# A decoder layer on one core: the last expert stage rebuilt, with V rows in fp32 in place of two-part sums at every third step

## The chip, the cores and the metric

The kernel runs on one core of a Trainium2 chip. The metric is the device time of one execution in microseconds (us); the figure of a kernel is the median of its runs. The profile is of one execution and gives times from the start of its span.

## What is computed

One step of a hybrid decoder layer for 1024 prompt tokens and 8 sample tokens: a mixer of two recurrent branches, an attention to 256 memory tokens, and a product-key expert layer (PEER), each added to the residual, then a final norm. The change touches the last part alone. For each token and each of 8 heads the 16 best of 16384 experts are picked, so 128 picks per token:

```python
idx  = ...                                # [token, 8 heads, 16 picks], from the two halves' scores
gate = softmax(top_s)
act  = gelu(einsum('td,thkd->thk', xb, expert_u[idx]))
coef = gate * act
out  = einsum('thk,thkd->td', coef, expert_v[idx])        # then x + out, RMSNorm
```

`expert_u` and `expert_v` are tables of 16384 rows of 1024 fp32 numbers (4 KB a row, 64 MB a table).

## The kernel before, in words

**Order.** The 1024 tokens are 8 blocks of 128, two to a group. `front(gi)` does all of a group up to its picks; `experts` (L1556) does the expert layer of the group before, beside it. The program is written in one order, and a planner at build time gives each engine a fixed list of instructions: where several are ready in its own model of time, the one that is earlier in the program goes first, and one that is ready may pass one that is not. At run time every engine goes through its list in order.

**The U side.** `u_step` (L1521) gathers, for one pick of each of 128 tokens, 128 rows of U into a buffer "U" by an indirect DMA that GpSimd issues (L1498), and multiplies and sums them with the tokens on VectorE (`dot`, L1502). In the fronts four picks of 16 are multiplied on GpSimd instead; in the tail all are dots on VectorE. A batch of 16 picks ends with Gelu and the gate; the factors are `cf`. So a block is 128 gathers.

**The V side, in two ways.** Blocks 0 to 3 go by gathers: `v_step` (L1534) gathers 128 V rows and adds them, times the factor, to `acc` on VectorE (L1550). Blocks 4 to 7 go in pairs by the whole table: `spread` (L1571) makes a matrix `cmat` [expert, token] of the factors, and `dense_sum` (L1612) multiplies it with the table in 128 steps of 128 V rows.

In `spread` there are 64 iterations of four tokens each for a pair. An iteration makes two 0/1 matrices by comparing a row of numbers with the picks' row and column numbers: `ra` on ScalarE (L1593, L1594) or VectorE (L1596) by turns, `rb` on VectorE (L1600), and GpSimd multiplies `rb` with the factors (`gtt`, L125). Four fp32 matmuls of 128x128 follow into a PSUM buffer "pp", and ScalarE copies the result to `cmat`. `cmat` is 128 KB per partition and has one buffer.

In `dense_sum` a step loads 128 V rows (0.5 MB, "Vx", issued by SyncE), splits the step's part of `cmat` and each half of the V rows in two float32r parts (ScalarE copies, L122; VectorE subtracts, L1626 and L1631; for one half of every second step GpSimd subtracts, L125), and adds three products for each of two halves and two blocks: 12 matmuls with 512 columns. The sums stay in four PSUM buffers ("pc", "pp").

**The tail.** The V rows of block 3 are left over for it (`beside`). After the last `front`, its pools are closed (`fronts.close`, L1724) and two pools are opened over their memory: `rows_late` with "U" (4 buffers), "Vx" and "cs", and `wd` with `cmat`, "vs" and "by". A tile of them waits until all of the old pool under it is released. Then the program is

```python
cmat = spread(late[:2])                   # blocks 4, 5
late += experts(prompts(chosen))          # U gathers and dots of blocks 6, 7
dense_sum(late[:2], cmat, ())
for z, k in beside[:VPOS]: v_step(...)    # 16 V steps of block 3
dense_sum(late[2:], spread(late[2:]), beside[VPOS:])     # blocks 6, 7; 112 V steps, one before each step
```

Blocks 6 and 7 get their picks at the end of the last `front` (`Best.pairs`, tile q3b).

Of the kernel before, what the change touches and what calls it, by code (L numbers as in the profile page):

```python
# [16 lines left out]
P = 128  # L17
D = 1024
NS = 8                      # sample tokens
# [6 lines left out]
NQ3, NG4, NXA, NK1, NU, NUT, NVX, NVS, NW, NAC = 26, 6, 2, 5, 5, 4, 4, 6, 3, 1  # L26
# [5 lines left out]
SPLIT = (0,)              # groups that go on by single blocks after their scans  # L32
POOL_DOTS = (2, 6, 10, 14)
NEARLY = 0
VPOS = 16
LATE_SLOTS = ()
ACT_A = range(0, 32, 2)
POOL_B = range(0, 32)
PB = 16                     # picks per batch of the expert phase
# [9 lines left out]
def decode_layer(ctx, tc, I, O):  # L49
    nc = tc.nc  # L50
    kept = ctx.enter_context(tc.tile_pool(name="kept", bufs=1))       # constants of every phase
    we = ctx.enter_context(tc.tile_pool(name="we", bufs=1))           # the experts' buffers
    fronts = ctx.enter_context(ExitStack())                           # what the fronts alone need
    rows_of = fronts.enter_context(tc.tile_pool(name="rows_of", bufs=1))      # gathered rows
# [44 lines left out]
    def pp():  # L99
        return pst("pp", 2)  # L100
# [26 lines left out]
    # ---------------------------------------------------------------- constants  # L127
# [6 lines left out]
    triu = const.tile([P, P], F32, name="triu")          # [k, l] = 1 for k <= l  # L134
    G.affine_select(out=triu, in_=ones, compare_op=OP.is_ge, fill=0.0, base=0,
                    pattern=[[1, P]], channel_multiplier=-1)
    maskg = const.tile([P, 2, 64], F32, name="maskg")    # [i mod 64, {i < t, i <= t}, t]
# [9 lines left out]
    sel4 = const.tile([P, 2, 32], F32, name="sel4")      # head of a channel in a pair of channel tiles  # L147
# [4 lines left out]
    sel4t = const.tile([P, 2, P], F32, name="sel4t")     # the same transposed, for every 32 partitions  # L152
# [5 lines left out]
    blk8 = kept.tile([P, NS], F32, name="blk8")         # [p, t] = 1 for p // 16 == t  # L158
# [15 lines left out]
    # parameters of a channel each, by columns  # L174
# [41 lines left out]
    V.tensor_scalar(alog, alog, -1.0, None, op0=OP.mult)     # a_head  # L216
# [8 lines left out]
    # state kept from group to group  # L225
    st = const.tile([P, D], F32, name="st")              # SSD, [n, (head, p)]
    G.memset(st, 0.0)
    rst = const.tile([P, 8, 64], F32, name="rst")        # RWKV, [(head of a pair, k), pair, v]
    G.memset(rst, 0.0)
    TT = [const.tile([P, 8, 64], F32, name=f"TT_{i}") for i in range(2)]     # inverses, transposed  # L230
# [7 lines left out]
    # kept in memory  # L238
# [7 lines left out]
    # ---------------------------------------------------------------- pieces  # L246
# [13 lines left out]
    class Parts:  # L260
        """1024 rows as the sum of two parts that float32r carries: 8 slices [128, n] of each."""
# [9 lines left out]
    def parts(wt):  # L271
        """Weights as the sum of two parts."""
# [8 lines left out]
    def three(out, a, b, first, last):  # L281
        """a.T @ b of operands in two parts."""
        for i, (x, y) in enumerate(((a[0], b[0]), (a[0], b[1]), (a[1], b[0]))):
            mm(out, x, y, first and i == 0, last and i == 2)

    def to_cols(x, n, dst, t0, wname=None):
        """x [n, 1024] into dst, 4 tiles [128, 2, T], by channels."""
# [38 lines left out]
    # ---------------------------------------------------------------- memory keys and values  # L326
    def memory():
        """By buffers of the experts, which are free until the first of them are chosen."""
        def cols4(dst, x, b):
            """x [128, 1024] into dst, by channels, with the norm's weights."""  # L330
# [54 lines left out]
    # ---------------------------------------------------------------- front of a group  # L385
# [6 lines left out]
    class Best:  # L392
        """The 16 best pairs of keys and their gates, for n rows and nh heads of each."""

        def __init__(self, n, nh):
# [9 lines left out]
                                   for i in range(2))                       # over i  # L405
# [8 lines left out]
        def add(self, sc, h):  # L414
            """Scores [n, 2 x 128] of head h."""
            for j in range(2):
                self.top16(sc[:self.n, j * P:(j + 1) * P], self.s[:self.n, h, j, :], self.i[:self.n, h, j, :])
# [32 lines left out]
    def front(gi):  # L450
        b0, nb = GROUPS[gi]
        sa, sm, sc_ = gi == 0, gi == 1, gi == 2     # the sample's input projection; up to its queries; the rest of it
# [7 lines left out]
        # normalized input, by channels  # L460
# [19 lines left out]
        # z, as 2 silu(z)  # L480
# [21 lines left out]
        # step widths  # L502
# [9 lines left out]
        def softplus(n, s):  # L512
            """dt of columns s (blocks) and n rows."""
# [23 lines left out]
        # causal convolution, by channels  # L537
        hc = t("hc", [P, 12, 3], 1)                      # what the rows before the group add to its first three
# [46 lines left out]
        # SSD scan  # L585
# [99 lines left out]
        # RWKV: projections, decayed operands by pairs of heads  # L685
# [24 lines left out]
        wc = t("wc", [P, 8, TMAX // 64], 2)              # decay of a whole chunk  # L710
# [21 lines left out]
        for q in range(4):  # L732
# [18 lines left out]
            for j in range(2):  # L751
# [4 lines left out]
                                       op0=OP.mult, op1=OP.mult)            # -kk  # L756
# [3 lines left out]
            V.scalar_tensor_tensor(ta[:, :, :TP], ta[:, :, :TP], 1.0, kk[:, :, :TP], op0=OP.add, op1=OP.mult)   # -2 b  # L760
# [22 lines left out]
            for j in range(2):  # L783
# [5 lines left out]
                for s in range(2):               # even heads (k, b), odd heads (b, k)  # L789
# [8 lines left out]
            # the triangles to invert  # L798
# [19 lines left out]
        # inverses of the triangles' diagonal blocks, a block to a partition  # L818
# [951 lines left out]
```

## Time and profile before

| | us |
|---|---|
| median of 3 runs (5183.37 to 5193.70) | 5188.58 |
| span of the profiled execution | 5188.6 |
| VectorE busy | 3990.9 (77%) |
| TensorE busy (matmuls) | 3838.1 (74%) |
| GpSimd busy | 3073.8 (59%) |
| ScalarE busy | 1864.4 (36%) |
| DMA, mean of the span | 251 GB/s |

The profiled execution's own time is its span. Engines: PE is TensorE (PEld its weight loads), DVE VectorE, ACT ScalarE, POOL GpSimd. A group names line, engine, operation and the tiles written and read; its columns are the count, the busy time, the mean of one in ns, and the idle time of the engine just before it with what ended most of that. The clock is TensorE's granted clock, 1.00 for 2.4 GHz and 0.50 for 1.2 GHz, as a mean of the stretch. An fp32 matmul stands in the trace as two instructions.

### The profile page before, as it was taken

What the parts mean: (1) busy time and instruction counts of PE and PEld (TensorE: products, weight loads), DVE (VectorE), ACT (ScalarE), POOL (GpSimd) and SP (SyncE); (2) the same over time, 40 slices, a digit from 0 to 9 for tenths busy, and PEclk for the clock granted to TensorE, in tenths of its full rate; (3) what the DMA queues carried; (4) which work ended last, traced back from release to release, by engine and by line L of the source; (5) the groups of instructions that cost most, each with busy time, mean ns of one, the idle gap of its engine ahead of it and who ended that gap; (6) DMA issues with size and microseconds to landing.
All of it is one profiled execution on the core that took longest, in us unless ns stands there. A gap on an engine that the chain in (4) does not pass through costs nothing.

```text
span 5188.6 us, 62002 instructions
## 1 busy us (share of the span) xinstructions
PE 3838.1 (74%) x20264; PEld 3063.8 (59%) x20264; DVE 3990.9 (77%) x7461; ACT 1864.4 (36%) x4475; POOL 3073.8 (59%) x2282
## 2 busy tenths in 40 slices
PE   7889867687977856978687467866756998047889
PEld 6677756565755734766566345655645776046667
DVE  4662397988766799887669987775799999689885
ACT  4544312232332212424332234243244554035445
POOL 2120045766767566567666776777667666678662
PEclk8988878888768868985788678758876999556999
DMA  3242778888878988997888678868825999865985
GB/s 96 91 129 85 230 250 305 271 288 288 275 241 313 320 278 296 306 311 229 314 326 265 227 256 273 271 221 301 283 71 177 350 348 329 275 202 190 308 285 166
DMA packets 586859, 1302.42 MB, mean 251 GB/s; under 512 B 80236, under 2 KB 326408, under 8 KB 586528
## 3 DMA queue, kind: packets, MB, share of 16 engines
q0 software_dynamic: 223488, 813.79, 45.3%
q1 hardware_dynamic: 363048, 484.67, 28.2%
q8 instruction: 160, 2.62, 0.2%
q14 instruction: 163, 1.34, 0.1%
HBM read 1268.49 MB, written 29.90 MB: 250 GB/s over the span
## 4 chain that ended last, share of the span: by engine, by line
PE 31%; DVE 30%; DMA 13%; issue 11%; POOL 9%; ACT 5%; SPq 1%; POOLq 0%; DVEq 0%; another core or an unknown queue 0%; ACTq 0%
PE pp L116 17%; PE pc L116 10%; DVE U L1502 6%; DMA U<-in_expert_u_dram,idx 5%; POOL U L1498 5%; DVE acc L1550 4%; DMA U<-in_expert_v_dram,idx 4%; POOL vs L125 2%; DVE q3b L438 2%; POOL U L125 1%; PE pv L116 1%; DVE vs L1600 1%; DMA w<-in_w_in_dram 1%; PE pg L116 1%; DVE q3b L441 1%
## 5 line engine op out<-in xcount | busy, mean ns | idle before, releaser
L1498 POOL DMA_INDIRECT U<-in_expert_u_dram,idx x1024 | 1215.9, 1187 | 745.3 <-DVE act L1502 245.7
L1502 DVE CUSTOM_DVE_ANT_0 U<-U,xa 128x1024 f32<-128x1024 f32 x840 | 1149.8, 1375 | 281.0 <-DMA U<-in_expert_u_dram,idx 264.6
L1498 POOL DMA_INDIRECT U<-in_expert_v_dram,idx x512 | 644.6, 1259 | 416.1 <-DVE acc L1550 117.9
L1550 DVE SCALAR_TENSOR_TENSOR acc<-U,cf,acc 128x1024 f32<-128x1024 f32 x512 | 748.2, 1461 | 167.3 <-DMA U<-in_expert_v_dram,idx 155.3
L116 PE MATMUL pp<-qw,w 128*128 128x256 f32 (+2 forms) x3024 | 764.8, 397 | 121.2 <-issue 43.4
L116 PE MATMUL pp<-w,qw 128*128 128x256 f32 (+1 forms) x2624 | 661.8, 401 | 151.0 <-DVE g L1040 40.6
L116 PEld LDWEIGHTS pp<-qw,w 128*128 128x128 f32 x3024 | 602.8, 210 | 242.2 <-issue 97.2
L116 PEld LDWEIGHTS pp<-w,qw 128*128 128x128 f32 (+1 forms) x2624 | 504.0, 195 | 279.5 <-DVE g L1040 47.7
L116 PE MATMUL pc<-vs,cs 128*128 128x512 f32 x1536 | 529.2, 398 | 78.1 <-POOL vs L125 46.6
L116 PE MATMUL pp<-vs,cs 128*128 128x512 f32 x1536 | 517.2, 391 | 0.0
L125 POOL TENSOR_TENSOR U<-U,xa 128x1024 f32<-128x1024 f32 x192 | 463.8, 2416 | 39.8 <-DMA U<-in_expert_u_dram,idx 36.8
L1526 ACT ACTIVATE U<-U 128x1024 f32<-128x1024 f32 x192 | 202.4, 1054 | 595.8 <-POOL U L125 588.5
L116 PEld LDWEIGHTS pc<-vs,cs 128*128 128x128 f32 x1536 | 282.7, 188 | 176.5 <-POOL vs L125 70.5
L125 POOL TENSOR_TENSOR vs<-Vx,vs 128x512 fp32r<-128x512 f32 x128 | 221.4, 1729 | 198.1 <-ACT vs L122 193.8
L122 ACT ACTIVATE vs<-Vx 128x512 fp32r<-128x512 f32 x512 | 304.4, 622 | 95.0 <-PE pp L116 93.9
L116 PEld LDWEIGHTS pp<-vs,cs 128*128 128x128 f32 x1536 | 289.1, 188 | 59.7
L116 PE MATMUL pp<-vs,vs 128*128 128x128 f32 x1024 | 231.0, 404 | 120.0 <-POOL vs L125 107.6
L1631 DVE TENSOR_TENSOR vs<-Vx,vs 128x512 fp32r<-128x512 f32 x384 | 296.0, 795 | 13.2 <-ACT vs L122 7.5
L116 PEld LDWEIGHTS pp<-vs,vs 128*128 128x128 f32 x1024 | 204.5, 299 | 146.5 <-POOL vs L125 141.6
L1626 DVE TENSOR_TENSOR cs<-cmat,cs 128x256 fp32r<-128x256 f32 x256 | 147.7, 577 | 106.6 <-ACT cs L122 102.1
L278 POOL TENSOR_TENSOR w<-w,U 128x1024 fp32r<-128x1024 f32 x31 | 74.5, 2403 | 258.2 <-ACT U L122 218.2
L122 ACT ACTIVATE cs<-cmat 128x256 fp32r<-128x256 f32 x256 | 106.9, 418 | 311.1 <-PE pp L116 293.7
(489 smaller groups left out, 7138.9 us busy)
## 6 DMA issues: line engine op xcount, KB each, us to landing
Vx<-in_expert_v_dram SPq DMA_DIRECT2D x256, 512.0 KB
w<-in_w_in_dram SPq DMA_DIRECT2D x124, 1024.0 KB
w<-in_w_pq_dram SPq DMA_DIRECT2D x40, 1024.0 KB
w<-in_w_out_dram SPq DMA_DIRECT2D x20, 1024.0 KB
w<-in_w_mq_dram SPq DMA_DIRECT2D x20, 1024.0 KB
w<-in_w_mo_dram SPq DMA_DIRECT2D x20, 1024.0 KB
U<-in_expert_u_dram,idx POOLq DMA_INDIRECT x1024
q<-kt_d SPq DMA_DIRECT2D x40, 256.0 KB
```

What stands on the lines that cost most here:

```text
L116: T.matmul(out, a, b, start=first, stop=last)
L122: S.activation(out, in_, AF.Copy, scale=scale if scale is not None else 1.0)
L125: G.tensor_tensor(out, a, b, op=op)
L278: (V if i else G).tensor_tensor(lo[:, k4, :], wt[:, k4, :], hi[i].bitcast(F32), op=OP.subtract)
L438: V.tensor_tensor(oh[:n], iota50[:n, None, :].to_broadcast([n, 8, NCAND]), posf[:n, h, k8].unsqueeze(2).to_broadcast([n, 8, NCAND]), op=OP ...
L441: V.tensor_reduce(idf[:n, h, k8], oh[:n], axis=AX.X, op=OP.add)
L1498: G.indirect_dma_start(out=dst, out_offset=None, in_=table, in_offset=bass.IndirectOffsetOnAxis(ap=idx, axis=0))
L1502: V.tensor_tensor_reduce(out=u, in0=u, in1=x, scale=1.0, scalar=0.0, op0=OP.mult, op1=OP.add, accum_out=out)
L1526: S.activation(u, u, AF.Copy, accum_out=z["act"][:, k:k + 1])
L1550: V.scalar_tensor_tensor(z["acc"], v, cf, z["acc"], op0=OP.mult, op1=OP.add)
L1626: V.tensor_tensor(cl[:, :nt], cmat[:, c, :nt], ch[:, :nt].bitcast(F32), op=OP.subtract)
L1631: (gtt if hf and c % 2 else lambda *a: V.tensor_tensor(*a[:3], op=a[3]))(vl, v[:, s], vh.bitcast(F32), OP.subtract)
```

## The change

- `NEARLY` 0 to 40: 40 V steps of block 3 stand before `fronts.close`, and use the fronts' five "U" buffers. `VPOS` 16 to 24: 24 more stand between the dense sums, and 64 beside the second.
- `experts` of blocks 6 and 7 stands before the first `spread`.
- `NUT` 4 to 5 buffers "U" in the tail; "by" moves to `rows_late`; both pools get `reuse_waits="tile"`: a tile waits for the old tiles that lie under it alone.
- `spread`: `rb` is made by four tensor_scalar of 128x128 on VectorE (compare and multiply in one), without GpSimd; the matmuls go to the PSUM buffers "tp" and "pg" by turns.
- `dense_sum`: in every third step (43 of 128) `cmat` and the V rows go into four plain fp32 matmuls, with no split; in the others VectorE does all subtractions.
- Comments are removed, with no effect on the program.

```diff
-NQ3, NG4, NXA, NK1, NU, NUT, NVX, NVS, NW, NAC = 26, 6, 2, 5, 5, 4, 4, 6, 3, 1
+NQ3, NG4, NXA, NK1, NU, NUT, NVX, NVS, NW, NAC = 26, 6, 2, 5, 5, 5, 4, 6, 3, 1
-NEARLY = 0
-VPOS = 16
+NEARLY = 40
+VPOS = 24
-POOL_B = range(0, 32)
+SPLIT_V = 3
@@ spread
-                p = pp()
-                if t0 // 4 in POOL_B:
-                    V.tensor_tensor(rb, iota[:, None, :].to_broadcast([P, 4, P]),
-                                    by[:, 1, t0:t0 + 4].unsqueeze(2).to_broadcast([P, 4, P]), op=OP.is_equal)
-                    gtt(rb, rb, by[:, 2, t0:t0 + 4].unsqueeze(2).to_broadcast([P, 4, P]), OP.mult)
-                else:
-                    for a in range(4):
-                        V.tensor_scalar(rb[:, a, :], iota, by[:, 1, t0 + a:t0 + a + 1], by[:, 2, t0 + a:t0 + a + 1],
-                                        op0=OP.is_equal, op1=OP.mult)
+                for a in range(4):
+                    V.tensor_scalar(rb[:, a, :], iota, by[:, 1, t0 + a:t0 + a + 1], by[:, 2, t0 + a:t0 + a + 1],
+                                    op0=OP.is_equal, op1=OP.mult)
+                p = tp() if t0 // 4 % 2 else pg()
@@ dense_sum
+            if c % SPLIT_V == 0:
+                for hf in range(2):
+                    for b in range(len(blocks)):
+                        mm(acc[b][hf], cmat[:, c, b * P:(b + 1) * P], v[:, hf * 512:(hf + 1) * 512], c == 0, c == P - 1)
+                continue
-                (gtt if hf and c % 2 else lambda *a: V.tensor_tensor(*a[:3], op=a[3]))(vl, v[:, s], vh.bitcast(F32),
-                                                                                       OP.subtract)
+                V.tensor_tensor(vl, v[:, s], vh.bitcast(F32), op=OP.subtract)
@@ program
-    rows_late = ctx.enter_context(tc.tile_pool(name="rows_late", bufs=1))     # not less than rows_of
-    for tag in ("U", "Vx", "cs"):
+    rows_late = ctx.enter_context(tc.tile_pool(name="rows_late", bufs=1, reuse_waits="tile"))
+    for tag in ("U", "Vx", "cs", "by"):
         pools[tag] = rows_late
-    pools["wd"] = ctx.enter_context(tc.tile_pool(name="wd", bufs=1))
-    cmat = spread(late[:2])
+    pools["wd"] = ctx.enter_context(tc.tile_pool(name="wd", bufs=1, reuse_waits="tile"))
     late += experts(prompts(chosen))
-    dense_sum(late[:2], cmat, ())
+    dense_sum(late[:2], spread(late[:2]), ())
```

## Rows read from the trace of the kernel before

**Rows 1.** Windows: PE, PEld, DVE, ACT, POOL busy (count), clock, DMA, GB/s
```profile
3780.00:3924.00 144.00, 89.54 (x402) 68.95 (x402) 143.47 (x420) 68.49 (x163) 87.68 (x71) 0.73 0.11 36
3924.00:4000.00 76.00, 45.87 (x192) 40.88 (x192) 70.34 (x88) 36.55 (x84) 65.64 (x52) 0.55 0.65 214
4000.00:4398.00 398.00, 364.00 (x1539) 281.39 (x1539) 366.10 (x600) 199.96 (x403) 243.94 (x199) 1.00 0.96 347
4398.00:4578.00 180.00, 0.00 (x0) 0.00 (x0) 119.42 (x197) 1.81 (x7) 114.34 (x97) 0.50 0.80 270
4578.00:4765.00 187.00, 128.94 (x549) 112.73 (x550) 175.73 (x161) 101.89 (x231) 154.20 (x111) 0.58 0.49 154
4765.00:5045.00 280.00, 234.17 (x976) 181.02 (x976) 243.83 (x285) 120.27 (x243) 188.96 (x121) 0.99 0.89 304
5045.00:5173.00 128.00, 126.75 (x564) 104.22 (x563) 71.20 (x117) 73.09 (x140) 31.02 (x24) 1.00 0.57 181
```

**Rows 2.** Timeline (start us, us, engine): last picks, first gather
```profile
3922.30 0.18 DVE L442 CAST idx<-q3b 128x64 int32<-128x64 f32 x1
3924.13 1.25 POOL L1498 DMA_INDIRECT U<-in_expert_u_dram,idx  x1
```

**Rows 3.** Groups of stage B: count, busy us, mean ns, idle before
```profile
L1502 DVE CUSTOM_DVE_ANT_0 U<-U,xa 128x1024 f32<-128x1024 f32 x131 | 160.0, 1222 | 2.7 <-DMA U<-in_expert_u_dram,idx 2.6
L1631 DVE TENSOR_TENSOR vs<-Vx,vs 128x512 fp32r<-128x512 f32 x192 | 128.3, 703 | 2.5
L1626 DVE TENSOR_TENSOR cs<-cmat,cs 128x256 fp32r<-128x256 f32 x128 | 92.1, 720 | 26.2 <-ACT cs L122 24.3
```

**Rows 4.** Waits of stage C: us in total, times, longest us
```profile
DVE U L1502 <- DMA U<-in_expert_u_dram,idx: 59.5, 75, 2.6
POOL U L1498 <- DVE act L1502: 49.4, 52, 2.1
```

**Rows 5.** Waits of stage E, while V rows are gathered
```profile
PEld pc L116 <- POOL vs L125: 59.8, 37, 2.1
```

**Rows 6.** Timeline of TensorE: the last matmuls of the second dense sum
```profile
5175.44 0.61 PE L116 MATMUL pp<-vs,cs 128*128 128x512 f32 x2
```

**Rows 7.** Groups of stage D, the second factor matrix
```profile
L125 POOL TENSOR_TENSOR vs<-vs,by 128x512 f32<-128x512 f32 x61 | 93.1, 1532 | 10.3 <-DVE vs L1600 9.6
L1600 DVE TENSOR_TENSOR vs<-iota,by 128x512 f32<-128x512 f32 x61 | 67.8, 1123 | 0.6 <-issue 0.6
L1596 DVE TENSOR_TENSOR vs<-niota,by 128x512 f32<-128x512 f32 x31 | 36.1, 1164 | 0.5 <-PE pp L116 0.5
L1550 DVE SCALAR_TENSOR_TENSOR acc<-U,cf,acc 128x1024 f32<-128x1024 f32 x45 | 68.0, 1511 | 0.0
L116 PE MATMUL pp<-vs,vs 128*128 128x128 f32 x512 | 121.7, 416 | 49.0 <-POOL vs L125 41.5 <-DVE xa L1643 3.7 <-ACT vs L1594 3.7
```

**Rows 8.** Groups of stage E, while V rows are gathered
```profile
L1631 DVE TENSOR_TENSOR vs<-Vx,vs 128x512 fp32r<-128x512 f32 x120 | 115.9, 988 | 0.1
L1550 DVE SCALAR_TENSOR_TENSOR acc<-U,cf,acc 128x1024 f32<-128x1024 f32 x83 | 110.4, 1330 | 0.9 <-DMA U<-in_expert_v_dram,idx 0.9
```

**Rows 9.** Groups of VectorE in the whole span: tensor_scalar from SBUF, alone
```profile
L704 DVE TENSOR_SCALAR q<-q 128x256 f32<-128x256 f32 x4 | 1.2, 288 | 0.5 <-ACT q L703 0.5
L1580 DVE TENSOR_SCALAR vs<-idx 128x128 int32<-128x128 int32 x4 | 0.8, 212 | 0.0
```

**Rows 10.** Tiles cmat and vs: minimum, median, maximum ns
```profile
L1626 DVE TENSOR_TENSOR cs<-cmat,cs x256: 408/425/1504, 4003.0 to 5170.9; 128x256 fp32r<-128x256 f32 x128
L1631 DVE TENSOR_TENSOR vs<-Vx,vs x384: 675/685/2423, 3999.9 to 5171.5; 128x512 fp32r<-128x512 f32 x192
```

**Rows 11.** Timeline of weight loads of fp32 matmuls with 512 columns
```profile
3794.03 0.09 PEld L116 LDWEIGHTS pv<-U,dgs 128*8 128x8 f32 x1 [0.34 <-issue]
3794.46 0.09 PEld L116 LDWEIGHTS pv<-U,dgs 128*8 128x8 f32 x1 [0.34 <-issue]
```

**Rows 12.** Windows of tile q3b, the picks: DVE, ACT, POOL busy
```profile
3780.00:3924.00 144.00, 72.69 (x324) 0.00 (x0) 30.02 (x24) 0.73 0.11 36
```

## The prediction

> **What bounds the kernel now.** I read the page first, for its span and its slices, then the windows of the tail, then in each window the groups and the waits. The profiled execution took 5188.6 us, and the median of the three runs is 5188.58 us, so the sum below is made against the one number. The edits begin where the picks of the last two blocks are being made, about 3780 us, so only 1409 us are in play [rows 1]. I call the stages A to E:
>
> A, 3780 to 4000: the first factor matrix (first `spread`) on VectorE, which is also choosing the last picks; the DMA share is 0.11 until 3924 [rows 1]. The last picks are written at 3922.30 and the first gather of the last blocks starts at 3924.13 [rows 2].
> B, 4000 to 4398: first dense sum. DMA is at 0.96 with 347 GB/s, PE is busy 364 of 398 us, VectorE 366: all three are nearly full. 131 dots of gathered rows went by in 398 us, about one per 128 V rows [rows 1, 3].
> C, 4398 to 4578: PE does nothing for 180 us. What is left of the gathers (97 instructions on GpSimd, two of them multiplications [rows 1]) goes round four buffers at 180 / 95 = 1.89 us each; VectorE waits for the gathers (59.5 us), the gathers for VectorE's dots (49.4 us) [rows 4], and DMA, at 0.80, is not full [rows 1].
> D, 4578 to 4765: second factor matrix. VectorE is busy 175.7 of 187 us; PE, which ran at its upper level of 2.4 GHz in B (granted clock 1.00), has fallen to the lower one for most of the stage (mean 0.58) after the idle of C [rows 1].
> E, 4765 to 5175: second dense sum. While V rows are gathered beside it 976 matmuls take 280 us, 3.44 us per 12 of them; without, 564 take 126.75 us of PE time, 2.70 us per 12 [rows 1]. The difference is PE waiting for GpSimd's subtraction (59.8 us of its weight loads) [rows 5].
> The last matmul starts at 5175.44 [rows 6], which leaves 13 us for the final norm.
>
> **The change part by part.**
> *GpSimd's arithmetic goes.* In D it multiplied 61 tiles in 93.1 us, and VectorE's two compares cost 67.8 + 36.1 = 104 us [rows 7], although such a compare is a 512-wide operation like the subtraction of B at 703 ns [rows 3]; in E the same subtraction takes 988 ns [rows 8]. What is added is 256 tensor_scalar of 128x128 per factor matrix: at 212 ns [rows 9] 54 us, at the 288 ns of the 256-wide row [rows 9] 74 us. I take 54, as the row has the right width (its data are integers). With 32 compares of about 0.70 us, VectorE's share of a matrix is 54 + 22 = 76 us in place of 104. In the dense sum VectorE's two kinds of subtraction cost 128.2 + 92.1 us in B [rows 3]; afterwards 85 of 128 steps need them, 85 x (0.425 + 2 x 0.685) = 153 us by the medians [rows 10].
>
> The Trainium skill weighs in twice here. Rows first: the 256-wide subtraction has a median of 425 and a maximum of 1504 ns [rows 10], so something holds VectorE up. The page "SBUF — State Buffer" ("Who interferes with whom") says that a VectorE instruction with two SBUF inputs contends with a GpSimd instruction that reads SBUF; the rows agree. The same section speaks against the new form: tensor_scalar may take both ports and shut GpSimd out, and the page's box on SWDGE has a descriptor-writing DMA grow from about 620 to 3100 ns beside such an operation. No row of this trace has tensor_scalars beside gathers. By that ratio the gathers beside the factor matrices would come every 3 us and not every 2, and as an estimate the sum would be some 10 us longer.
>
> *Every third 128 V rows in fp32.* It drops the copies and subtractions of 43 steps, and its four matmuls run as eight passes of 512 columns. The trace has such passes: weight loads of fp32 512-column matmuls follow each other in 0.43 us [rows 11]. So a step is 8 x 0.43 = 3.44 us in place of 2.70, and a dense sum that PE alone bounds takes 43 x 3.44 + 85 x 2.70 = 377 us in place of 346. This part costs 32 us of PE per sum, on the path wherever PE is the bound.
>
> *40 V gathers move ahead of the fronts' end.* They are queued on GpSimd's DMA queue behind the last U gathers of the group before and ahead of the new ones, and meet an idle DMA until 3924. They cost VectorE 40 x 1.33 = 53 us [rows 8] beside 73 us for the picks [rows 12].
>
> *The last blocks' gathers go ahead of the first factor matrix, with five buffers and tile-wise waits.* Now block 6's gathers wait for the old pool to be empty at 3922; afterwards for its own picks and its own tiles. Five buffers would make 1.89 x 4 / 5 = 1.5 us per gather, which is also what the 0.524 MB of a gather (128 rows of 4 KB) take at the 347 GB/s of B [rows 1]. Queued behind these dots on VectorE is now the first factor matrix, and behind that PE's first dense sum: it must start later than 4000. Let N be the dots done before it starts. VectorE from 3780: picks and small ones 78, V steps 53, matrix 76, dots N x 1.29 (1.22 and the read of the accumulator): start = 3987 + 1.29 N. N is not in the trace; its ends are about 32, as now, and all 256, if the planner keeps strictly to the program's order. For the choice: in D, with four buffers, 45 V steps came beside 61 to 64 iterations of the matrix [rows 7], though 16 of them stood ahead of it in the program; so a place in the order did not make gathers come faster than their buffers came round. With five buffers that is 0.9 per iteration, 57 dots, and some before the matrix begins: N = 70, start about 4077.
>
> *First dense sum.* Beside it lie 128 loads of V and 256 - N gathers, 0.524 MB each: with N = 70, 314 x 0.524 / 347 GB/s = 474 us, more than PE's 377. End: 4077 + 474 = 4551. With N = 32 it is 4028 + 531 = 4559, with N = 130 4155 + 384 = 4539: as long as DMA bounds the sum, a dot moved ahead costs 1.29 and saves 1.5 us, so the end hardly depends on N up to 130. I take 4550. C is gone, and what is late next is the DMA.
>
> *Second factor matrix.* It can't begin before the first sum has released the one factor buffer. VectorE: 76 us and some 53 V steps of 1.33, 70 us: 146. ScalarE was busy 102 us in all of D [rows 1], PE 122 us with this [rows 7]. I take 146 us (122 to 187): 4696.
>
> *Second dense sum.* 35 V steps are left beside it. B, with a gather per step, took 398 / 128 = 3.11 us against 2.70, 0.4 us each: 377 + 14 = 391 us (377, to the 410 of now plus 32). End 5087, and with 13 us for the norm 5100. The terms that I could only bound from above (compares at 0.70, tensor_scalar back to back at their full duration) lean to the long side; I forecast **5090 us**, -1.9%, and for this case alone 5030 to 5150.
>
> **Rivals.**
> *Strict order (slower).* VectorE takes the dots whenever one is there, the matrix gets what is left, and all 256 dots lie before the first dense sum: start 3987 + 256 x 1.29 = 4317. With the remaining V steps beside it the sum takes 377 + 25, ends at 4719; matrix 122, sum 377, norm 13: 5231, say 5200 to 5260. It decides from N of about 130 on, where each dot costs 1.29 us and saves nothing; the time of now is passed at N of about 225. For it: five buffers bring a gather every 1.5 us, and a dot takes 1.29 of these on VectorE. Against: in B the dots also stood ahead of the dense sum in the program and came only one per step [rows 3].
> *DMA never idle (faster than forecast).* If the 40 V gathers, at 1.9 us each, end at 3856, the others flow from there on and the matrix fits in between, the first sum's end is set by bytes: (256 + 128) x 0.524 / 347 = 580 us, 4435; with 146, 391 and 13 that gives 4985, and 4940 to 5030 with the bounds.
> *The change doesn't do what it says.* The waits of E and the stretch of D are of the queue's making and stay (187 us, and 410 + 32 us): from 4550 on 187 + 442 + 13 gives 5192, no change; anything between lies at 5150 to 5192.
>
> **How the numbers follow.** Forecast case 0.58, DMA never idle 0.15, near no change (5150 to 5200) 0.10, strict order 0.17. About 0.2% (10 us) is what a measurement of this kernel tells from no change, as the three runs lie within 5183.37 to 5193.7. Below 5178: 0.58 + 0.15 + half of 0.10 and a little less for the tails, 0.78; within 0.2%: 0.06; above: 0.16. The range 4985 to 5215 leaves out a part of the fast case and the upper half of the strict one.
>
> **What would show it.** Right: no stretch without matmuls of more than 20 us between the first dense sum and the second factor matrix; the first dense sum starting between 4030 and 4160 with a DMA share over 0.9 and lasting over 430 us; V gathers in 3780 to 3924; subtractions near 0.69 us; fp32 steps of 3.4 us; the last sum under 400 us. Wrong: a first dense sum that starts after 4250, or one that starts early and is followed by PE waiting for the last gathers again. The prediction would also be wrong if tensor_scalar slowed the gathers' issue so far that GpSimd, at 244 of 398 us in B [rows 1], became the bound.

## The result, and the profile after

| | before | after |
|---|---|---|
| median, us (4 runs each, side by side) | 5191.14 (5183.37 to 5196.92) | 5019.59 (5014.13 to 5025.69) |
| ratio, 95% interval | | 0.9677 (0.9661 to 0.9693) |
| profiled execution, us (span) | 5188.58 (5188.6) | 5017.32 (5015.3) |

The changed kernel is 3.2% faster. The forecast was 5090 us, -1.9%: the sign was right and the size too small. The windows of the same stages, cut at the changed kernel's own borders, answer rows 1. The columns are busy us and count of PE, PEld, DVE, ACT and POOL, then clock, DMA share and GB/s.

```profile
3780.00:3905.00 125.00, 21.01 (x71) 10.68 (x69) 119.42 (x336) 8.82 (x22) 73.75 (x65) 0.57 0.63 197
3905.00:4098.00 193.00, 134.12 (x519) 110.05 (x519) 190.72 (x478) 98.26 (x228) 127.63 (x95) 0.55 0.80 257
4098.00:4490.00 392.00, 386.43 (x1360) 254.56 (x1361) 334.94 (x605) 130.72 (x265) 188.86 (x165) 1.00 1.01 396
4490.00:4615.00 125.00, 88.00 (x555) 76.48 (x553) 123.69 (x327) 97.37 (x237) 32.56 (x30) 0.92 0.48 145
4615.00:4740.00 125.00, 122.28 (x432) 80.61 (x433) 112.26 (x139) 41.87 (x82) 73.69 (x55) 1.00 0.99 388
4740.00:5002.00 262.00, 262.00 (x946) 176.21 (x944) 110.99 (x181) 91.29 (x175) 0.00 (x0) 1.00 0.55 176
```

Up to 3905 VectorE makes the last picks and the 40 early V steps. From 3905 to 4098 it makes the first factor matrix and takes the dots of some 90 gathered rows. The first dense sum runs to 4490, with PE busy in 386 of its 392 us. The stretch C, in which PE did nothing for 180 us [rows 1], is gone: the second matrix follows at once, 125 us instead of 187, and the second sum takes 387 us instead of 410. The norm takes 13 us as before. The last picks and the first gather of U stand 20 us earlier than in rows 2 (timeline of the changed kernel: start, us, engine):

```profile
3902.09 0.18 DVE L442 CAST idx<-q3b 128x64 int32<-128x64 f32 x1
...
3905.08 0.98 POOL L1498 DMA_INDIRECT U<-in_expert_u_dram,idx  x1 [5.67 <-DVE acc L1550]
```

The groups of VectorE and of GpSimd's DMA issues in the second matrix (count, busy us, mean ns, idle before) answer rows 7:

```profile
L1599 DVE TENSOR_SCALAR vs<-iota,by 128x128 f32<-128x128 f32 x256 | 72.6, 362 | 1.3 <-ACT by L122 1.3
L1550 DVE SCALAR_TENSOR_TENSOR acc<-U,cf,acc 128x1024 f32<-128x1024 f32 x29 | 37.2, 1283 | 0.0
L1498 POOL DMA_INDIRECT U<-in_expert_v_dram,idx x30 | 32.6, 1085 | 105.7 <-DVE vs L1599 56.8 <-DVE acc L1550 22.9 <-ACT by L122 19.1
L1596 DVE TENSOR_TENSOR vs<-niota,by 128x512 f32<-128x512 f32 x32 | 21.9, 685 | 0.0
```

The compare of 512 went from 1164 to 685 ns, the V step from 1511 to 1283. In the first dense sum the two subtractions stand at 694 and 424 ns, where rows 3 had 703 and 720:

```profile
L1502 DVE CUSTOM_DVE_ANT_0 U<-U,xa 128x1024 f32<-128x1024 f32 x166 | 201.7, 1220 | 27.8 <-DMA U<-in_expert_u_dram,idx 24.2 <-issue 2.6
L1631 DVE TENSOR_TENSOR vs<-Vx,vs 128x512 fp32r<-128x512 f32 x170 | 114.5, 694 | 8.6 <-ACT vs L122 7.4
L1626 DVE TENSOR_TENSOR cs<-cmat,cs 128x256 fp32r<-128x256 f32 x85 | 35.9, 424 | 18.0 <-ACT cs L122 14.0 <-PE pp L116 2.6 <-issue 0.4
```

### The profile page after: what moved, and what is told of

Same layout as the page of the kernel before. It is cut to its first block, busy times and chain, and to the rows that moved or that the text cites. A ratio compares the mean times of both kernels' runs of the same rounds, so it can differ in the third digit from the quotient of the medians.

```text
span 5015.3 us, 60096 instructions
## 1 busy us (share of the span) xinstructions
PE 3854.3 (77%) x19920; PEld 2973.4 (59%) x19920; DVE 3786.5 (75%) x7715; ACT 1732.6 (35%) x4215; POOL 2685.6 (54%) x2026
## 4 chain that ended last, share of the span: by engine, by line
DVE 32%; PE 27%; DMA 14%; issue 12%; POOL 9%; ACT 4%; SPq 1%; POOLq 0%; another core or an unknown queue 0%; DVEq 0%; ACTq 0%
PE pp L116 15%; PE pc L116 8%; DVE U L1502 7%; POOL U L1498 6%; DMA U<-in_expert_v_dram,idx 5%; DVE acc L1550 5%; DMA U<-in_expert_u_dram,idx 4%; DVE vs L1599 2%; POOL U L125 2%; DVE q3b L438 2%; PE pv L116 1%; PE pg L116 1%; DMA q<-kt_d 1%; DVE q3b L441 1%; PE tp L116 1%
## 5 line engine op out<-in xcount | busy, mean ns | idle before, releaser
L116 PE MATMUL pc<-vs,cs 128*128 128x512 f32 x1020 | 413.9, 460 | 7.6 <-DVE vs L1631 6.3
L116 PE MATMUL pp<-vs,cs 128*128 128x512 f32 x1020 | 344.0, 392 | 0.0
L1631 DVE TENSOR_TENSOR vs<-Vx,vs 128x512 fp32r<-128x512 f32 x340 | 230.5, 693 | 80.6 <-ACT vs L122 74.0
L122 ACT ACTIVATE vs<-Vx 128x512 fp32r<-128x512 f32 x340 | 205.9, 623 | 152.5 <-PE pp L116 88.2
L116 PEld LDWEIGHTS pc<-vs,cs 128*128 128x128 f32 x1020 | 189.8, 188 | 102.3 <-issue 47.2
L116 PEld LDWEIGHTS pp<-vs,cs 128*128 128x128 f32 x1020 | 191.8, 188 | 66.0 <-issue 27.9
L116 PE MATMUL tp<-vs,vs 128*128 128x128 f32 x512 | 110.5, 369 | 153.4 <-DVE vs L1599 142.8
L116 PE MATMUL pp<-q,w 128*128 128x128 f32 (+1 forms) x1024 | 191.7, 345 | 6.9 <-ACT q L122 5.8
L116 PEld LDWEIGHTS tp<-vs,vs 128*128 128x128 f32 x512 | 91.7, 259 | 171.1 <-ACT vs L1594 99.9
L116 PEld LDWEIGHTS pp<-q,w 128*128 128x128 f32 x1024 | 165.4, 206 | 22.9 <-ACT q L122 8.3
```

Source lines behind the costliest of these rows:

```text
L116: T.matmul(out, a, b, start=first, stop=last)
L122: S.activation(out, in_, AF.Copy, scale=scale if scale is not None else 1.0)
L1631: V.tensor_tensor(vl, v[:, s], vh.bitcast(F32), op=OP.subtract)
```

## The experiments

Each was timed beside its own runs of the kernel before; their medians lie between 5169 and 5183 us, so the ratios are what is compared across groups. The first seven change one or two things in the changed kernel, the next three build its parts up from the kernel before, and the last two take up the order and the tile `by` once more.

### GpSimd's arithmetic put back (a_gpsimd)

```diff
-                for a in range(4):
-                    V.tensor_scalar(rb[:, a, :], iota, ..., op0=OP.is_equal, op1=OP.mult)
+                V.tensor_tensor(rb, ..., op=OP.is_equal)
+                gtt(rb, rb, ..., OP.mult)
-                V.tensor_tensor(vl, v[:, s], vh.bitcast(F32), op=OP.subtract)
+                (gtt if hf and c % 2 else lambda *a: V.tensor_tensor(*a[:3], op=a[3]))(vl, ...)
```

> The changed kernel with one part undone: GpSimd multiplies in the factor matrices and subtracts for one half of the odd steps again. Theory: VectorE's operations stretch again (685 to 1000 ns and more), each matrix takes some 30 to 40 us longer, and PE waits for GpSimd in the steps with gathers beside, some 20 us per sum: about 5120 us. Rival (order and buffers did it, GpSimd's part was hidden): under 5040 us.

Measured: 5175.34 us, ratio 0.9981 (0.9968 to 0.9994). The direction is the theory's, the size larger: 3.0 of the 3.2% gained, some 156 us, are lost again. Windows of both matrices and both sums, then groups of the second matrix:

```profile
3933.00:4174.00 241.00, 129.47 (x510) 109.50 (x508) 234.43 (x302) 95.93 (x224) 216.30 (x159) 0.54 0.69 212
4174.00:4600.00 426.00, 394.50 (x1358) 259.02 (x1359) 340.12 (x539) 130.48 (x264) 271.61 (x199) 0.98 0.94 351
4610.00:4783.00 173.00, 131.72 (x547) 113.32 (x545) 170.46 (x149) 94.04 (x218) 153.85 (x112) 0.57 0.53 161
4783.00:5179.00 396.00, 389.08 (x1374) 259.60 (x1375) 177.16 (x253) 133.63 (x257) 100.55 (x77) 0.98 0.61 213
```
```profile
L125 POOL TENSOR_TENSOR vs<-vs,by 128x512 f32<-128x512 f32 x62 | 93.6, 1516 | 9.9 <-DVE vs L1598 9.2
L1596 DVE TENSOR_TENSOR vs<-niota,by 128x512 f32<-128x512 f32 x31 | 35.4, 1143 | 2.3 <-PE pg L116 2.3
```

Against the changed kernel the stages are longer by 48 (241 and 193), 34, 48 and 9 us; the rest of the profiled difference (177 us, as the profiled execution is the slowest of the ten) is a later start (3933 against 3905) and the 10 us between first sum and second matrix. The same compare (L1596) takes 1143 ns beside GpSimd's multiplications and 685 without them. In the first sum something else is added: TensorE waits for GpSimd's own subtraction (us in total, times, longest):

```profile
PE pc L116 <- POOL vs L125: 29.3, 19, 3.0
```

### The fp32 steps taken out (a_nofp32)

```diff
-            if c % SPLIT_V == 0:
+            if False:
```

> The changed kernel with one part undone: no plain fp32 steps, all 128 steps in two parts, all subtractions on VectorE. Theory: VectorE bounds the first sum, 128 x 1.80 + 166 x 1.29 = 444 us in place of 392, and the second gains 20 to 31 us on PE: net +20 to +30, about 5040 us. Rival (PE alone bounds both sums, fp32 steps cost 31 us each): 4955 us.

Measured: 5034.83 us, ratio 0.9704 (0.9674 to 0.9734), near the theory's 5040. But the interval overlaps that of the changed kernel (0.9661 to 0.9693), so the plain steps as a whole are worth a few tenths of a per cent at most. Windows of the first and the second sum:

```profile
4110.00:4533.00 423.00, 377.02 (x1537) 282.67 (x1538) 402.31 (x732) 192.54 (x393) 173.57 (x166) 0.99 0.97 364
4662.00:5025.00 363.00, 355.97 (x1551) 289.51 (x1552) 291.73 (x447) 199.16 (x383) 92.10 (x56) 1.00 0.74 262
```

VectorE, at 402 of 423 us, bounds the first sum without plain steps. With them VectorE is at 335 of 392 and PE bounds it: they are worth 31 us there. In the second sum, where PE is the bound either way, they cost 24. That leaves 7 us; 12 more of the profiled difference are a later start of the first sum (4110 against 4098), which no run explains.

### The old order (a_order), and the old waits (a_pool)

```diff
-    late += experts(prompts(chosen))
-    dense_sum(late[:2], spread(late[:2]), ())
+    cmat = spread(late[:2])
+    late += experts(prompts(chosen))
+    dense_sum(late[:2], cmat, ())
```
```diff
-    rows_late = ctx.enter_context(tc.tile_pool(name="rows_late", bufs=1, reuse_waits="tile"))
+    rows_late = ctx.enter_context(tc.tile_pool(name="rows_late", bufs=1))
-    pools["wd"] = ctx.enter_context(tc.tile_pool(name="wd", bufs=1, reuse_waits="tile"))
+    pools["wd"] = ctx.enter_context(tc.tile_pool(name="wd", bufs=1))
```

> The changed kernel with one part undone: the first factor matrix stands ahead of the gathers of the last blocks again. Theory (the path is the start of the first dense sum, then PE; gathers come at their buffers' pace wherever they stand): dense sum from about 4000, over at 4390, some 50 dots left then at 1.5 to 2 us each, of which half hide behind the second matrix; 4930 to 5000 us, not slower than the changed kernel (5020). Rival (the new order is what removed the hole): the hole without matmuls returns with 80 us or more, over 5080 us.

> The changed kernel without the word that lets the late pools' tiles wait for single earlier tiles instead of for the whole pool they replace. Theory (the first late gather stands behind the 40 V gathers in GpSimd's queue and the factor matrix behind the last picks in VectorE's, so neither waits for the pool): within 10 us of the changed kernel, 5005 to 5035. Rival (that wait is part of the gain): first U gather after 3920 in the trace, over 5040 us.

Measured: a_order 5012.51 us, ratio 0.9670 (0.9647 to 0.9694); a_pool 5018.49, 0.9677 (0.9654 to 0.9701). Both stand at the changed kernel's 0.9677: undone one at a time, with the early V gathers in place, neither the new order nor the tile-wise waits are worth anything measurable. What I had ranked as the change's leading part, the gathers put ahead of the matrix in the program, is not a cause.

### No early V gathers (a_nearly0)

```diff
-NEARLY = 40
+NEARLY = 0
```

> The changed kernel with one part undone: no V steps ahead of the fronts' end, 104 beside the second dense sum in place of 64. Theory: the gathers of the last blocks start some 35 us earlier (they stood behind the 40 on GpSimd), the first sum some 50 us earlier, and 40 more V steps hide under a second sum that PE bounds: about 4965 us. Rival (filling the idle DMA at 3800 to 3900 is a part of the gain): 40 x 1.3 = 52 us longer, about 5070 us.

Measured: 4960.06 us, ratio 0.9570 (0.9546 to 0.9594), the theory's value: the 40 early V steps cost 1.1%, about 56 us. Their group in the changed kernel, 3780 to 3905:

```profile
L1550 DVE SCALAR_TENSOR_TENSOR acc<-U,cf,acc 128x1024 f32<-128x1024 f32 x40 | 61.7, 1542 | 0.0
```

And the kernel without them, timeline and window of the second dense sum, which now has 104 V steps beside it:

```profile
3847.77 0.98 POOL L1498 DMA_INDIRECT U<-in_expert_u_dram,idx  x1 [0.15 <-issue]
3848.26 0.20 DVE L442 CAST idx<-q3b 128x64 int32<-128x64 f32 x1
```
```profile
4560.00:4949.00 389.00, 385.89 (x1374) 257.09 (x1375) 267.50 (x359) 131.80 (x257) 114.98 (x95) 1.00 0.79 297
```

The steps held VectorE for 62 us ahead of the last picks, and the first gather of U came 57 us later (3905 against 3848). Beside the second sum, which PE bounds, the same steps are free: 389 us against 387.

### Four buffers (a_nut4)

```diff
-NQ3, NG4, NXA, NK1, NU, NUT, NVX, NVS, NW, NAC = 26, 6, 2, 5, 5, 5, 4, 6, 3, 1
+NQ3, NG4, NXA, NK1, NU, NUT, NVX, NVS, NW, NAC = 26, 6, 2, 5, 5, 4, 4, 6, 3, 1
```

> The changed kernel with four buffers for the late gathers of U instead of five. Theory (the gathers of U run at the pace at which buffers come free): with five buffers 256 gathers take 555 us, 2.17 us each, that is 10.8 us a buffer; with four 2.7 us each and 694 us, so they end near 4600 instead of 4460, 110 us behind the first dense sum, and the kernel takes 5060 to 5130 us. Rival (they run at the pace of GpSimd's issue and VectorE's sums, not of the buffers): 5005 to 5035 us, no hole.

Measured: 5031.64 us, ratio 0.9705 (0.9679 to 0.9732), 0.3% slower, with intervals that overlap; the time is the rival's, and the mechanism is half the theory's. The gathers of U did slow down, from 3912 to 4553, 2.50 us each against 2.18. But their end cost little: 36 of the dots ran inside the second matrix, which made it 155 us long and needed no hole. Group and window of that matrix:

```profile
L1502 DVE CUSTOM_DVE_ANT_0 U<-U,xa 128x1024 f32<-128x1024 f32 x36 | 43.5, 1216 | 1.2 <-DMA U<-in_expert_u_dram,idx 1.2
```
```profile
4476.00:4631.00 155.00, 109.44 (x548) 93.07 (x546) 146.55 (x380) 99.21 (x232) 55.66 (x50) 0.72 0.58 186
```

### A version with less fp32 (x_best)

No early V gathers, and plain steps every third in the first sum but every sixth in the second.

```diff
-NEARLY = 40
+NEARLY = 0
-            if c % SPLIT_V == 0:
+            if c % every == 0:          # 3 in the first sum, 6 in the second
```

> The changed kernel with no early V gathers, and plain fp32 steps every third in the first dense sum as now but every sixth in the second. Theory (first sum: TensorE and VectorE in balance; second: TensorE alone is the bound and 22 plain steps cost it 16 us instead of 32): 4960 as without early V gathers, less 16 to 25: 4930 to 4950. Rival (the 104 V steps left to the second sum, 1.28 us each on VectorE, make VectorE its bound once more steps have subtractions): 4955 or more.

Measured: 4952.00 us, ratio 0.9562 (0.9533 to 0.9591). It is no faster than a_nearly0 beyond the intervals. Where V rows are gathered, VectorE is nearly full, as the rival has it (window inside the second sum):

```profile
4550.00:4650.00 100.00, 94.26 (x377) 68.86 (x378) 94.86 (x135) 43.78 (x87) 57.20 (x40) 1.00 0.94 358
```

### From the other side: parts added to the kernel before (b_nogp, b_nogp5, b_nogp5by)

b_nogp takes GpSimd's arithmetic out of the kernel before, b_nogp5 gives it the fifth buffer too, and b_nogp5by also moves the tile `by`. Each has the edits of the one before it.

```diff
 # b_nogp
-                    gtt(rb, rb, by[:, 2, t0:t0 + 4]..., OP.mult)
+                    # four V.tensor_scalar, and all subtractions on V, as in the change
 # b_nogp5
-NQ3, ..., NUT, ... = 26, 6, 2, 5, 5, 4, 4, 6, 3, 1
+NQ3, ..., NUT, ... = 26, 6, 2, 5, 5, 5, 4, 6, 3, 1
 # b_nogp5by
-    for tag in ("U", "Vx", "cs"):
+    for tag in ("U", "Vx", "cs", "by"):
```

> The kernel before with one part of the change alone: GpSimd's multiplications in the factor matrix and its subtractions in the dense sums go to VectorE; four buffers of gathers, no early V gathers, no plain fp32 steps. Theory (GpSimd's arithmetic is the loss): putting it back into the changed kernel cost 156 us, so taking it out of the kernel before gives most of the gain alone, also because this kernel has no early V gathers to pay for: 5000 to 5060 us, first dense sum about 420 us (VectorE-bound, as in the kernel without plain fp32 steps), no hole of over 40 us behind it. Rival (the parts only work together, four buffers hold the gathers back): the hole behind the first dense sum stays at over 100 us and the time is over 5100 us.

> The kernel before without GpSimd's arithmetic, as above, and with a fifth buffer for the late gathers of U, nothing else. Theory (the hole behind the first dense sum ends with the last gather, and the gathers run at the pace at which buffers come free): 256 gathers at 2.17 us instead of 2.45 end 71 us earlier, near 4492, so the hole shrinks from 258 to about 190 us and the kernel takes 5005 to 5040 us. Rival (their pace is that of VectorE's sums and of the DMA beside the dense sum): 5080 to 5105 us.

Measured: b_nogp 5093.53 us, ratio 0.9818 (0.9785 to 0.9852); b_nogp5 5068.19, 0.9793 (0.9773 to 0.9812). Taken out alone, the arithmetic gives 1.8%, between theory and rival, and the hole is there as the rival has it. Windows of b_nogp: first matrix, hole, second matrix, second sum:

```profile
3814.00:3937.00 123.00, 86.98 (x509) 75.35 (x507) 121.62 (x449) 90.68 (x219) 18.60 (x16) 0.87 0.00 1
...
4324.00:4582.00 258.00, 7.59 (x36) 7.09 (x34) 165.68 (x284) 12.65 (x30) 158.83 (x129) 0.51 0.81 272
4582.00:4698.00 116.00, 78.95 (x517) 68.63 (x516) 115.96 (x309) 90.08 (x219) 27.76 (x27) 0.95 0.41 132
4698.00:5079.00 381.00, 360.86 (x1552) 289.60 (x1552) 330.96 (x490) 198.19 (x385) 158.28 (x98) 0.99 0.85 308
```

The first matrix ends 63 us earlier than before, but VectorE does it ahead of the last picks. So DMA moves 1 GB/s meanwhile, the gathers of U start at 3937 and end at 4563, and the hole grows from 180 to 258 us. The saved time ran into the hole. The fifth buffer ends the gathers at 4520 and shrinks the hole to 177 us, but the first sum beside the denser gathers grows from 383 to 421 us, so only some 0.25% is left of it, which the intervals don't separate from nothing. Window of b_nogp5's first sum, with VectorE at 391:

```profile
3941.00:4362.00 421.00, 373.53 (x1534) 281.51 (x1535) 391.45 (x713) 192.74 (x391) 166.03 (x161) 0.99 0.98 363
```

What then brought the gathers early in the changed kernel? Neither order nor waits (a_order, a_pool). Another candidate that touches the first matrix is `by`: by the program it lies in `rows_late` over the memory of the fronts' gathered rows and must wait until that is released.

> The kernel before without GpSimd's arithmetic and with five buffers, as above, and one name moved: the tile by of the factor matrix goes to the pool that takes over the memory of the gathered rows. Theory (what lets the late gathers start early is not the program's order but this: by then waits until that memory is released, which is after the last picks, so VectorE's list has the picks ahead of the matrix): first gather of U near 3850 instead of 3937, matrix about 3855 to 4040 with gathers beside it, first dense sum about 420 us, no hole, 4975 to 5005 us. Rival (the place of by has no weight): 5055 to 5080 us, hole as before.

Measured: 5001.88 us, ratio 0.9664 (0.9633 to 0.9696), against 0.9793 without: one name in a list is worth 1.3%. Timeline and windows (first matrix, first sum, rest of the hole):

```profile
3843.30 0.20 DVE L442 CAST idx<-q3b 128x64 int32<-128x64 f32 x1
...
3844.35 0.98 POOL L1498 DMA_INDIRECT U<-in_expert_u_dram,idx  x1 [1.69 <-ACT by L122]
```
```profile
3849.00:4030.00 181.00, 114.55 (x509) 101.02 (x508) 176.30 (x446) 95.92 (x225) 103.02 (x83) 0.63 0.75 249
4030.00:4455.00 425.00, 376.48 (x1539) 283.08 (x1539) 402.21 (x737) 192.81 (x393) 176.80 (x169) 0.99 0.98 365
4455.00:4478.00 23.00, 6.45 (x28) 6.18 (x29) 14.88 (x33) 10.41 (x21) 8.13 (x8) 0.61 0.76 280
```

The matrix now waits for the picks and not the picks for the matrix; gathers flow 93 us earlier, beside it, and the hole is 23 us. Three of the change's edits (no arithmetic on GpSimd, the fifth buffer, the place of `by`) thus reach the changed kernel's ratio.

### Order and `by` without the early V gathers (x_order0, x_by_new)

x_order0 is a_nearly0 with the old order of a_order. x_by_new is a_nearly0 with `by` in its old pool.

```diff
 # x_by_new
-    for tag in ("U", "Vx", "cs", "by"):
+    for tag in ("U", "Vx", "cs"):
```

> The changed kernel without early V gathers and with the old order, the first factor matrix ahead of the late experts' gathers. Theory (the order does matter, and the 40 early V gathers covered it: with them VectorE reaches the last picks before it is free for the matrix in either order): without them the matrix runs from about 3814 to 3937 with no gathers beside it, as in the kernel before without GpSimd's arithmetic, the picks of the last block come behind it, the gathers of U start near 3937 instead of 3848, end near 4492, well behind the first dense sum (about 4335), and the kernel takes 5000 to 5030 us. Rival (the order is worth nothing here either): 4945 to 4975 us, first gather of U before 3870.

> The changed kernel without early V gathers, its new order kept, but by back in its old pool. Theory (by's place, not the program's order, decides when the picks are ready): VectorE does the matrix ahead of the last picks although the program has it behind the gathers; first gather of U near 3937 instead of 3848, a hole of 150 to 200 us behind a first dense sum that ends near 4330, and 5020 to 5060 us. Rival (the new order, or the other parts, bring the gathers early): 4950 to 4975 us.

Measured: x_order0 4956.56 us, ratio 0.9573 (0.9557 to 0.9589), beside 0.9570 of a_nearly0. My theory of a covered effect falls: the first gather starts at 3861, and the order is worth nothing without the V gathers too. x_by_new: 4966.23 us, 0.9605 (0.9577 to 0.9632), 0.35% over a_nearly0, with intervals that overlap. Here the theory is right in its first half and wrong in the time. The gathers do start late, and the first matrix runs without them, as in b_nogp:

```profile
3928.53 1.39 POOL L1498 DMA_INDIRECT U<-in_expert_u_dram,idx  x1
```
```profile
3811.00:3935.00 124.00, 86.63 (x509) 74.45 (x507) 121.89 (x452) 91.19 (x220) 23.55 (x21) 0.89 0.03 11
3943.00:4335.00 392.00, 387.73 (x1367) 255.45 (x1367) 339.42 (x612) 132.52 (x265) 201.25 (x171) 1.00 1.01 398
4339.00:4562.00 223.00, 115.47 (x549) 95.81 (x547) 201.15 (x474) 99.64 (x234) 113.73 (x95) 0.64 0.72 241
4562.00:4949.00 387.00, 384.77 (x1374) 256.28 (x1375) 286.24 (x376) 131.84 (x257) 137.39 (x112) 1.00 0.84 322
```

But there is no hole ahead of the second matrix: it starts at 4339 on block 6, with the last dots inside it (group of that stretch). TensorE's wait for them, 63 us in one piece, lies between its two blocks:

```profile
L1502 DVE CUSTOM_DVE_ANT_0 U<-U,xa 128x1024 f32<-128x1024 f32 x84 | 102.3, 1222 | 15.3 <-DMA U<-in_expert_u_dram,idx 14.7
4494.44 3.77 PE L116 MATMUL pv<-finw,ident 8*128 8x128 f32 x16 [62.73 <-DVE xa L1511]
```

In b_nogp5 the second matrix had no dot in it. So the changed kernel has two covers for the late gathers: an early start (`by`), and a second matrix that can begin among them. Which edit gives the second cover was not run alone, but the two traces tell. First b_nogp5, then x_by_new (timelines: start, us, engine):

```profile
4534.98 1.29 DVE L1642 TENSOR_TENSOR xa<-pp,xa 128x512 f32<-128x512 f32 x2 [6.83 <-DMA xa<-x_d]
4535.81 3.62 PE L116 MATMUL pp<-vs,vs 128*128 128x128 f32 x16 [6.58 <-DVE xa L1642]
```
```profile
4338.48 1.30 PE L116 MATMUL pg<-vs,vs 128*128 128x128 f32 x8 [3.58 <-ACT vs L1594]
4503.44 1.29 DVE L1642 TENSOR_TENSOR xa<-pp,xa 128x512 f32<-128x512 f32 x2 [3.08 <-DMA xa<-x_d]
```

L1642 reads the first sum's result of block 5 out of the PSUM buffers "pp", of which there are two. It needs a tile "xa", of which there are two as well, and the load of that tile is issued only after the last dot, at 4527.7 in b_nogp5 and 4496.7 in x_by_new. Where the matrix writes to "pp", as in the kernel before, its first matmul must follow that read. Where it writes to "tp" and "pg", it started 165 us ahead of it. (Most of TensorE's recorded wait in the hole of b_nogp5, 162.5 us, stands at the norm of block 4, which its list has ahead of the matrix there and which waits behind the dots too; the read of "pp" is the wait that ends last.) So the hole was not the gathers alone: it was the gathers, and a result that waited behind them in the buffers of the next stage. What the move to "tp" and "pg" is worth by itself no run shows.

## Why the prediction was right in sign and short in size

By its own sum the prediction said 5100; the profiled execution's span is 5015.3. The 85 us come from three terms.

*First dense sum, 474 us predicted, 392 measured: the term that failed.* I read B's DMA share of 0.96 at 347 GB/s as a full engine and divided bytes by it. With the 90 dots that were done ahead of it the same price gives 294 x 0.524 / 347 = 444 us, still 52 too long. A window of 40 us inside the changed kernel's first sum shows that DMA can do more:

```profile
4180.00:4220.00 40.00, 39.02 (x140) 25.72 (x139) 34.09 (x61) 13.41 (x27) 19.08 (x18) 1.00 1.03 409
```

So 347 GB/s was no ceiling, and PE bounds the new sum: 43 x 3.44 + 85 x 2.70 = 377 us stood in the prediction as PE's time, and of the 392 measured PE was busy 386. In the stretch 4740 to 5002 PE is busy throughout; 16 of its 946 rows are a norm's (2.3 us), and the other 930 are 87.2 steps (32 rows are two split steps and a plain one), 8.94 us per three, so a plain step is 8.94 - 2 x 2.70 = 3.54 us, close to the 3.44 of the sum. The Trainium skill has the higher rate: the page "Perfetto Trace Analysis", section "Roofline", says that one core alone can pull more than the per-core share of 358 GB/s that it gives for HBM, with some 120% as the practical ceiling. The trace agrees with its 409 GB/s, 114% of that share; the sum had left that out.

*Start of it, 4077 predicted, 4098 measured.* N was 90 (256 less the 166 of the first sum) and not 70, 20 x 1.29 = 26 us. The V steps took 62 us and not 53. The tensor_scalars have 358 to 362 ns each, more than my upper bound, but overlap: in the timeline of the second matrix eight in a row stand in 2.15 us, 0.27 us each, 69 us a matrix where I took 54. The picks' tile q3b took 57 us of VectorE in this stretch, where the sum had 78 for the picks and small ones. These four add up to 29 us; the measured 21 is less, and neighbouring instructions overlap in the trace.

```profile
4541.61 2.15 DVE L1599 TENSOR_SCALAR vs<-iota,by 128x128 f32<-128x128 f32 x8
```

The remark that a dot moved ahead hardly shifts the sum's end had the DMA bound under it and fell with it.

*Second matrix, 146 predicted, 125 measured.* 29 V steps were beside it and not 53 (24 x 1.28 = 31 us less); the tensor_scalars took back 15.

*Second sum, 391 predicted, 387 measured,* and the norm, 13 and 13. The size of the sum was right partly by luck: 14 of its 391 us were for 35 V steps at 0.4 us each. About 60 lay beside it, and with about 100 in a_nearly0 it took 389 us, so a V step costs such a sum next to nothing.

*The whole.* The measured 5020 us lies below the forecast case's own 5030 to 5150 and inside the outer range. Of the signs that were to show it right all came but one, the length of the first sum (over 430 us was said, 392 came).

*The parts.* That GpSimd's arithmetic stretches VectorE was the reading of rows 7, 8 and 10, and a_gpsimd shows it, though two different ratios belong to it: 1.8% alone, 3.0% with the rest of the change in place, since alone its gain runs into the hole. The 32 us of PE time per sum for the plain steps came out as 24 (second sum, a_nofp32); that they unload VectorE in the first sum, 31 us, I had not counted. The early V gathers I priced at 53 us of VectorE, and they stood in my start of 3987, but I did not ask what they cost where they came from: nothing. The order and the tile-wise waits, to which I gave the earlier start of the gathers, do nothing; I passed over the move of `by` without a cost, and that is where it comes from. The move to "tp" and "pg" I passed over too, and so I did not ask what kept PE waiting through all of C: by the trace the wait that ended last was the one for the read of "pp" (L1643 there), behind the last dot at 4585 (timeline of the kernel before):

```profile
4592.55 5.41 PE L116 MATMUL pp<-vs,vs 128*128 128x128 f32 x24 [3.68 <-DVE xa L1643]
```

*The rivals.* Strict order needed all dots ahead of the first sum: about 90 of 256 were, and a_order shows that the program's order does not matter. DMA never idle, 4985, had the sum set by bytes at 347 GB/s as well, with a gather start of 3856. The time lies between it and the forecast, but PE sets the sum's end in the changed kernel, so that case was not the one either. No change: the waits went, as rows 5 has no counterpart in the changed kernel's sums.

*The rule on the shared port.* The Trainium skill's page "SBUF — State Buffer", "Who interferes with whom", was weighed against tensor_scalar; the growth from 620 to 3100 ns stands in that page for a tensor_copy. Gathers' issues beside 256 tensor_scalars in the first matrix, then beside none in the first sum:

```profile
L1498 POOL DMA_INDIRECT U<-in_expert_u_dram,idx x95 | 128.7, 1355 | 71.0 <-DVE vs L1599 36.6 <-DVE act L1502 21.1 <-issue 7.3
L1498 POOL DMA_INDIRECT U<-in_expert_u_dram,idx x162 | 186.4, 1151 | 178.0 <-DVE act L1502 170.1 <-issue 6.7 <-DVE vs L1631 0.9
```

In the second matrix, with as many tensor_scalars, they took 1085 ns. So nothing near the fivefold growth. The other rule of that section, two-input VectorE against GpSimd reading, fits a_gpsimd's 1143 against 685 ns.

## What to carry to other kernels

Take a rate as a ceiling only from a stretch in which no other engine is near full; a DMA share of 0.96 beside two nearly full engines says nothing of what DMA could do. Before work is moved ahead, ask what it costs where it is (beside a sum that another engine bounds it may be free) and which small thing is queued behind it in its new place. When a change has many edits, look for what makes the planner place the late producer: here one tile's pool was worth 1.3% in one setting (0.35%, not clear of noise, in another), and the program's order nothing in any. When an engine stands idle, ask which buffer its next instruction writes, and who still has to read it.

## What the runs showed of the hardware that I had not expected

DMA moved 409 GB/s at a share of 1.03, where 0.96 stood beside 347 [rows 1]. A tensor_scalar of 128x128 fp32 with two scalars per partition lasts 358 ns but follows its like in 0.27 us. The V step, a three-operand VectorE operation of 1024, takes 1283 ns beside gathers alone and 1542 in the stretch where GpSimd multiplies for the picks. PE's granted clock in the second matrix does not follow from the idle time ahead of it: it was 0.58 behind 180 idle us [rows 1] and 0.92 in the changed kernel, where the first sum ran up to it, but also 0.95 in b_nogp behind a hole of 258 us and 0.57 in a_gpsimd behind 7.5 idle us. It goes with the length of the matrix: 0.92 and 0.95 where it took 125 and 116 us, 0.72 at 155 (a_nut4), 0.57 to 0.64 at 173 to 223 (a_gpsimd, the kernel before, x_by_new). Which of the two is the cause no run shows.
